# Up projections of a two-layer encoder: the first unit of every group makes its high products in eights ahead of its low ones, not in pairs with them

## The chip, the cores and the metric

One core of one Trainium2 chip runs the whole program. The metric is the device time of one execution in microseconds (us); smaller is better. Products run on TensorE (PE in the profile), weight loads on the same engine beside them (PEld), the other work on VectorE (DVE), ScalarE (ACT) and GpSimd (POOL), and SyncE (SP) issues nearly all DMAs.

## The reference

The input is x (1, 256, 2048) in float32, with a condition c and parameters of two layers. Per layer: a norm, modulated by c, an input projection that feeds four mixers, an output projection, a post-norm, and then a gated feed-forward part. Only that last part is touched:

```
h = layer_norm(x) * (1.0 + scale_f) + shift_f
up = h @ w_up[l]                       # (256, 2048) @ (2048, 2 * 5632)
gate, val = split(up, 2)
gate = causal_dwconv(gate, w_conv, b_conv)   # width 3
y = (silu(gate) * val) @ w_down[l]
x = layer_norm(ALPHA * x + (1.0 + gate_f) * y, ...)
```

The up projection has 11264 columns per layer over 2048 rows; it is 42% of the kernel's span.

## The kernel before, in words

**High and low parts.** A float32 weight is used as two float32r parts: a high part, made by an ACT cast (line 344), and a low part, what is left, made by a DVE subtraction (line 345, which reads the high part). The activations hT are split in the same way. One weight block of 128 rows x 128 columns gives two products (both through the helper at line 117): a *high product*, the high weights with 512 moving columns (256 tokens of the high activations beside 256 of the low ones), and a *low product*, the low weights with the 256 high activations. Both add into one accumulator of PSUM.

**Groups and units.** `group2` makes 512 output columns: four accumulators c0 to c3 of 128 channels each, summed over 16 blocks of rows. A group has four *units* of four row blocks: one DMA of 1 MB (tile wraw, 4 buffers), then two *tiles* of two row blocks each, so two casts (whi, 4 buffers) and two subtractions (wlo, 4 buffers), then 16 high and 16 low products. With four buffers of each and two a unit, the casts and subtractions of a unit two further on wait until PE has read the tiles of this one for the last time.

**The stage.** `ffn_up` makes gate groups (g_c in the profile) and value groups (v_c) in turn, 10 gate groups (the first gate group of a layer is made otherwise, by `first_group`) and 11 value groups in each of the two layers: 42 groups. A layer's input projection uses `group2` too, in layer 1 alone, and there with `apart=True`: groups Dg, Da, U, Cc, Ch, E. Units are issued in a software pipeline (`stream`): the loads, casts and subtractions of a unit are written ahead of the products of the one before. The Tile framework's scheduler then orders each engine's instructions by its own estimate of when they can start; PE, DVE and ACT then run their own instructions in that order.

**Order of products in a unit.** Without `apart`, a unit makes two halves, c0 and c1 first, then c2 and c3, and in a half each high product is followed by its low one: high, low, high, low, eight of each. With `apart`, unit 0 makes the same two halves, but in each the eight high products and then the eight low ones; its later units make all sixteen high ones and then all sixteen low ones.

**What else runs beside it.** When a group has ended, ACT copies half of each accumulator out (line 1391) and DVE adds the other half (1398 or 1428). Gate groups put a convolution (line 1420) and a SiLU (1423) in the background. In layer 0, DVE also multiplies the modulation weights of later steps (tile wmod, line 193, 2.3 us each). Near the end of a layer's up projections the gated activations are split for the down projection (lines 365 and 366, tile a), whose products are called d.

Of the kernel before, what the change touches and what calls it, by code (L numbers as in the profile page):

```python
# [86 lines left out]
def encoder_kernel(ctx: ExitStack, tc: tile.TileContext, A: dict, consts: bass.AP, out: bass.AP):  # L87
# [25 lines left out]
    def acc_tile(name):  # L113
        return accp.tile([P, 512], F32, tag="acc", name=name)

    def mm(o, lhsT, rhs, start, stop):
        pe.matmul(o, lhsT, rhs, start=start, stop=stop, skip_group_check=True)  # L117
# [196 lines left out]
    def weights(w, k0, nk, c0, width, exact=False, spare=0):  # L314

        w, l = w
        n = nk * width
        if exact:
            parts, per = [], min(nk, max(1, 1024 // width))
            for k in range(0, nk, per):  # L320
                if spare:
                    r = slot("wexact")
                else:
                    tag = ("whi", "wlo")[exact_turn[0] % 2]
                    exact_turn[0] += 1
                    r = splitp.tile([P, 1024], F32, tag=tag, name="wexact")
                m = per * width
                nc.sync.dma_start(out=r[:, :m], in_=w.take(m, rows_of(l, k0 + k, per, c0, width)))
                for j in range(per):
                    parts.append((r[:, j * width : (j + 1) * width], None))  # L330
            return parts
        raw = raw_tile("wraw")
        nc.sync.dma_start(out=raw[:, :n], in_=w.take(n, rows_of(l, k0, nk, c0, width)))
        per = max(1, 1024 // width)
        parts = []
        for k in range(0, nk, per):
            m = per * width
            if k < spare:
                hi, lo = slot("thi", F32R), slot("tlo", F32R)
            else:  # L340
                hi = splitp.tile([P, 1024], F32R, tag="whi", name="whi")
                lo = splitp.tile([P, 1024], F32R, tag="wlo", name="wlo")
            r = raw[:, k * width : k * width + m]
            held(act.copy(hi[:, :m], r), "cast")  # L344
            i = dve.tensor_tensor(out=lo[:, :m], in0=r, in1=hi[:, :m].bitcast(F32), op=ALU.subtract)  # L345
            held(i, "split")
            for j in range(per):
                parts.append((hi[:, j * width : (j + 1) * width], lo[:, j * width : (j + 1) * width]))
        return parts
# [69 lines left out]
    def group2(w, c0, name, then, bg=0, spare=0, apart=False):  # L419


        nk = 4
        box = {}

        def products(item, u):
            if u == 0:
                box["c"] = [acc_tile(f"{name}_c{i}") for i in range(4)]
                box["h"] = list(hT)
            if apart:
                for part in (range(0, 2), range(2, 4)) if u == 0 else (range(0, 4),):  # L430
                    for low in (0, 1):
                        for k, w_k in enumerate(item):
                            kt = u * nk + k
                            both = box["h"][kt // 2][2][:, kt % 2, :, :]
                            for i in part:
                                o, a = box["c"][i], w_k[low][:, i * P : (i + 1) * P]
                                if low:
                                    mm(o[:, :S], a, both[:, 0, :], False, kt == KT - 1)
                                else:
                                    mm(o, a, both.rearrange("p h t -> p (h t)"), kt == 0, False)  # L440
                return
            for part in (range(0, 2), range(2, 4)):
                for k, (hi, lo) in enumerate(item):
                    kt = u * nk + k
                    both = box["h"][kt // 2][2][:, kt % 2, :, :]
                    for i in part:
                        o = box["c"][i]
                        off = slice(i * P, (i + 1) * P)
                        mm(o, hi[:, off], both.rearrange("p h t -> p (h t)"), kt == 0, False)
                        mm(o[:, :S], lo[:, off], both[:, 0, :], False, kt == KT - 1)  # L450

        def load(u):
            return weights(w, u * nk, nk, c0, 512, False, spare if u == 0 else 0)

        return KT // nk, load, products, lambda: then(box["c"]), bg

    def latent_group(w, c0, name, then, hF=None, bg=0):
# [1201 lines left out]
```

## Time and profile before

| | |
|---|---|
| median of 3 runs | 2212.66 us (2212.3, 2212.66, 2218.01) |
| profiled execution | 2212.3 us, span of its instructions 2210.5 us |
| mean granted TensorE clock | 0.996 |
| PE busy | 2184.5 us (99% of the span), 10852 matmuls |
| PEld busy | 1792.5 us (81%) |
| DVE busy | 1701.8 us (77%) |
| ACT busy | 1076.1 us (49%) |
| HBM | 604.17 MB read, 274 GB/s over the span |

How to read it: the ends of matmuls are modelled, and a matmul is shown longer than the time until the next one starts. So what a product costs is read from the distance between the starts of runs of products (the chain and the timeline), not from the mean duration of one. A few matmul records are missing, which merges two neighbours in the timeline and moves no start of a run that is recorded.

### The profile page before, as it was taken

The numbers are of one execution on the slowest core, as the hardware profiler recorded it, in microseconds if no ns is written. First come the engines' busy times: TensorE is split into PE (matmuls) and PEld (weight loads), VectorE is DVE, ScalarE is ACT, GpSimd is POOL, SyncE is SP. The second block draws the span as 40 slices with busy tenths as digits, with TensorE's granted clock in tenths as the row PEclk, the third lists the DMA queues.
The fourth block names the chain that finished last, engine by engine and source line by source line (L and its number), as shares of the span: only waits on it lengthen the run. The fifth ranks groups of instructions, "written<-read, shape, count | busy, mean of one in ns | idle before, by whom it ended". The sixth has DMA issues, their size and how long they took to land. (4 is left out here: it accounts for less than half of the span.)

```text
span 2210.5 us, 28322 instructions
## 1 busy us (share of the span) xinstructions
PE 2184.5 (99%) x10852; PEld 1792.5 (81%) x10852; DVE 1701.8 (77%) x2265; ACT 1076.1 (49%) x1652; POOL 21.9 (1%) x38
## 2 busy tenths in 40 slices
PE   8999999999999999999999999999999999999997
PEld 6776865588888888888877988868888888888886
DVE  5657997798898888989968988877765656575776
ACT  3132730655454545545665455465444544454553
POOL 0000000000000000000000000000000000000000
PEclk9999999999999999999999999999999999999999
DMA  9999889598888988898857547856765555565553
GB/s 392 417 375 391 353 331 392 214 343 322 334 315 319 327 326 318 335 342 325 285 218 304 184 153 263 326 195 245 267 210 190 188 191 191 191 210 192 192 196 144
DMA packets 94730, 608.15 MB, mean 275 GB/s; under 512 B 10689, under 2 KB 10881, under 8 KB 29313
## 3 DMA queue, kind: packets, MB, share of 16 engines
q1 hardware_dynamic: 94466, 606.31, 74.3%
q8 instruction: 85, 1.39, 0.2%
q14 instruction: 51, 0.42, 0.0%
q10 hardware_dynamic: 128, 0.03, 0.0%
HBM read 604.17 MB, written 2.13 MB: 274 GB/s over the span
## 5 line engine op out<-in xcount | busy, mean ns | idle before, releaser
L345 DVE TENSOR_TENSOR wlo<-wraw,whi 128x1024 fp32r<-128x1024 f32 (+1 forms) x608 | 728.5, 1212 | 294.4 <-ACT whi L344 279.2
L344 ACT CAST whi<-wraw 128x1024 fp32r<-128x1024 f32 (+1 forms) x608 | 631.5, 1045 | 637.0 <-PE g_c L117 214.2
L117 PE MATMUL v_c<-hT,whi 128*128 128x512 f32 x1408 | 489.2, 392 | 0.0
L193 DVE SCALAR_TENSOR_TENSOR wmod<-wmod,crep 128x2048 f32<-128x2048 f32 x192 | 438.0, 2285 | 59.6 <-DMA wmod<-in_w_mod_dram 58.9
L117 PE MATMUL g_c<-hT,whi 128*128 128x512 f32 x1280 | 444.6, 392 | 0.0
L117 PE MATMUL v_c<-hT,wlo 128*128 128x256 f32 x1408 | 392.1, 279 | 0.0
L117 PE MATMUL d<-whi,a 128*128 128x512 f32 x1344 | 386.4, 389 | 0.0
L117 PE MATMUL g_c<-hT,wlo 128*128 128x256 f32 x1280 | 356.5, 278 | 0.0
L117 PEld LDWEIGHTS v_c<-hT,whi 128*128 128x128 f32 x1408 | 263.6, 187 | 59.1
L117 PEld LDWEIGHTS d<-whi,a 128*128 128x128 f32 x1344 | 252.0, 188 | 52.3
L117 PEld LDWEIGHTS g_c<-hT,whi 128*128 128x128 f32 x1280 | 239.7, 187 | 54.1
L117 PEld LDWEIGHTS v_c<-hT,wlo 128*128 128x128 f32 x1408 | 265.3, 188 | 0.1
L117 PEld LDWEIGHTS g_c<-hT,wlo 128*128 128x128 f32 x1280 | 241.1, 188 | 0.0
L117 PE MATMUL d<-wlo,a 128*128 128x512 f32 x672 | 232.9, 389 | 0.0
L117 PEld LDWEIGHTS d<-wlo,a 128*128 128x128 f32 x672 | 126.1, 188 | 26.3
L365 ACT CAST a<-g 128x512 fp32r<-128x512 f32 x132 | 81.3, 617 | 63.7 <-PE d L117 63.1
L366 DVE TENSOR_TENSOR a<-g,a 128x512 fp32r<-128x512 f32 x132 | 88.7, 684 | 5.1 <-ACT a L365 5.1
L117 PE MATMUL o<-whi,a 128*128 128x512 f32 x320 | 91.1, 391 | 0.0
L503 PE MATMUL first<-wexact,hN 128*128 128x512 f32 x192 | 85.5, 596 | 0.5
L1420 DVE SCALAR_TENSOR_TENSOR u<-g,par,u 128x254 f32<-128x254 f32 (+1 forms) x176 | 73.8, 476 | 0.0
L117 PEld LDWEIGHTS o<-whi,a 128*128 128x128 f32 x320 | 59.9, 188 | 12.8 <-ACT whi L344 0.4
L503 PEld LDWEIGHTS first<-wexact,hN 128*128 128x128 f32 x192 | 35.3, 190 | 40.3 <-issue 35.2
(311 smaller groups left out, 2171.8 us busy)
## 6 DMA issues: line engine op xcount, KB each, us to landing
wmod<-in_w_mod_dram SPq DMA_DIRECT2D x192, 1024.0 KB, 7.1
wraw<-in_ffn_w_up_dram SPq DMA_DIRECT2D x168, 1024.0 KB, 5.1
wraw<-in_ffn_w_down_dram SPq DMA_DIRECT2D x88, 1024.0 KB, 4.9
wexact<-in_w_in_dram SPq DMA_DIRECT2D x64, 512.0 KB, 11.3
wraw<-in_w_in_dram SPq DMA_DIRECT2D x24, 1024.0 KB, 6.8
wraw<-in_w_out_dram SPq DMA_DIRECT2D x22, 1024.0 KB, 5.7
wexact<-in_w_out_dram SPq DMA_DIRECT2D x20, 512.0 KB, 11.6
wexact<-in_ffn_w_up_dram SPq DMA_DIRECT2D x16, 512.0 KB, 5.4
```

Source lines behind the costliest of these rows:

```text
L117: pe.matmul(o, lhsT, rhs, start=start, stop=stop, skip_group_check=True)
L193: i = dve.scalar_tensor_tensor(out=raw, in0=raw, scalar=1.0, in1=crep, op0=ALU.mult, op1=ALU.mult, accum_out=col)
L344: held(act.copy(hi[:, :m], r), "cast")
L345: i = dve.tensor_tensor(out=lo[:, :m], in0=r, in1=hi[:, :m].bitcast(F32), op=ALU.subtract)
L365: last_cast[0] = act.copy(hi, src).ins.name
L366: dve.tensor_tensor(out=lo, in0=src, in1=hi.bitcast(F32), op=ALU.subtract)
L503: i = pe.matmul(ps, hN[kt // 4][:, kt % 4, t * P : (t + 1) * P], parts[kt], start=kt == 0, stop=kt == KT - 1, skip_group_check=True,)
L1420: dve.scalar_tensor_tensor(out=u[:, sh:], in0=x[:, : S - sh], scalar=col(k, j), in1=u[:, sh:], op0=ALU.mult, op1=ALU.add)
```

## The change

One condition. In `group2`, the branch that makes high products ahead of low ones is taken in unit 0 of every group, also where `apart` is off. Only the up projections call `group2` with `apart` off, so in their 42 groups unit 0 goes from pairs to eight high and eight low products, twice. Units 1 to 3 of these groups stay in pairs. The number of instructions, their operands and all DMAs stay.

```
@@ -426,7 +426,7 @@
             if u == 0:
                 box["c"] = [acc_tile(f"{name}_c{i}") for i in range(4)]
                 box["h"] = list(hT)
-            if apart:
+            if apart or u == 0:
                 for part in (range(0, 2), range(2, 4)) if u == 0 else (range(0, 4),):
                     for low in (0, 1):
                         for k, w_k in enumerate(item):
```

On PE, in the second half of unit 0 of the second gate group of layer 0: whi_2545 and wlo_2546 are the high and low parts of the unit's first tile, whi_2549 the high part of its second one, and c2 and c3 are accumulators.

```order
 L117 MATMUL g01_c2_2614<-hT_2326,whi_2545 128x512
+L117 MATMUL g01_c3_2615<-hT_2326,whi_2545 128x512
+L117 MATMUL g01_c2_2614<-hT_2326,whi_2545 128x512
+L117 MATMUL g01_c3_2615<-hT_2326,whi_2545 128x512
+L117 MATMUL g01_c2_2614<-hT_2327,whi_2549 128x512
+L117 MATMUL g01_c3_2615<-hT_2327,whi_2549 128x512
+L117 MATMUL g01_c2_2614<-hT_2327,whi_2549 128x512
+L117 MATMUL g01_c3_2615<-hT_2327,whi_2549 128x512
 L117 MATMUL g01_c2_2614<-hT_2326,wlo_2546 128x256
-L117 MATMUL g01_c3_2615<-hT_2326,whi_2545 128x512
 L117 MATMUL g01_c3_2615<-hT_2326,wlo_2546 128x256
-L117 MATMUL g01_c2_2614<-hT_2326,whi_2545 128x512
```

All eight high products now stand ahead of the first low one; so PE is done with the two high tiles earlier in the unit than before, and with the first low tile later.

On DVE, in layer 0, where it makes the low parts of the third gate group (g02): wlo_3058 and wlo_3062 are the two low tiles of that group's unit 2, which take over buffers that unit 0 has read, and wmod is a multiplication of modulation weights.

```order
 L345 TENSOR_TENSOR wlo_3058<-wraw_3055,whi_3057 128x1024
+L345 TENSOR_TENSOR wlo_3062<-wraw_3055,whi_3061 128x1024
 L193 SCALAR_TENSOR_TENSOR wmod_3097,sums_0_5_2367<-wmod_3097,crep_104 128x2048
-L345 TENSOR_TENSOR wlo_3062<-wraw_3055,whi_3061 128x1024
 L345 TENSOR_TENSOR wlo_3103<-wraw_3100,whi_3102 128x1024
```

One subtraction moves ahead of one multiplication. The rest of DVE's order is the same but for one more such exchange, with a split of activations near the end of layer 1.

On ACT, near the end of layer 1's up projections: whi_15459 is the second high tile of unit 2 of the last value group, a_15656 a part of the activations of the down projection, and g_15376 a SiLU of the gate.

```order
 L344 CAST whi_15455<-wraw_15453 128x1024
-L365 CAST a_15656<-g_11857 128x2x256
+L344 CAST whi_15459<-wraw_15453 128x1024
 L1423 ACTIVATE g_15376<-u_15443 128x256
 L1423 ACTIVATE g_15376<-u_15448 128x256
-L344 CAST whi_15459<-wraw_15453 128x1024
+L365 CAST a_15656<-g_11857 128x2x256
 L365 CAST a_15693<-g_11857 128x2x256
```

The cast moves ahead of two SiLUs, and the first split of the activations behind them. A handful of other groups have a cast exchanged with a SiLU in the same way. The orders of POOL and SP are unchanged.

More of the change, by code (lines that the diff above doesn't have):

```diff
@@ L428, in products @@
                 box["h"] = list(hT)
-            if apart:
+            if apart or u == 0:
                 for part in (range(0, 2), range(2, 4)) if u == 0 else (range(0, 4),):
```

## The prediction

> **What bounds the kernel now.** I read the page first, for the busy shares; PE is busy in 99% of the span and no other engine passes 77%.
>
> ```profile
> span 2210.5 us, 28322 instructions
> PE 2184.5 (99%) x10852; PEld 1792.5 (81%) x10852; DVE 1701.8 (77%) x2265; ACT 1076.1 (49%) x1652; POOL 21.9 (1%) x38
> ```
>
> A busy share doesn't say whether PE waits in the stage that is changed, so next comes the chain that ended last, in order of time. From 1492.59 us it is PE almost without a break; these are some of the pieces of layer 1's up projections (start, length, what).
>
> ```profile
> 1515.46 22.19 PE g_c L117 x128
> 1537.64 22.19 PE v_c L117 x128
> ...
> 1914.82 22.19 PE g_c L117 x128
> 1937.01 22.19 PE v_c L117 x128
> 1959.19 0.11 PE ps_gate L239
> 1959.30 239.42 PE d L117 x1056
> ```
>
> Every group takes the same 22.19 us, whatever DVE and ACT did meanwhile, and each starts when the one before ends. That is a stage in which PE sets the time and waits for nobody. For both layers I checked it by the stages' windows (length, busy time of PE, PEld, DVE, ACT, POOL, granted clock, DMA share, GB/s): PE is busy in 466.99 of 467.00 us in layer 0, too, where DVE and the DMAs have more to do, and the clock is full.
>
> ```profile
> 433.00:900.00 467.00, 466.99 (x2696) 408.11 (x2695) 412.97 (x510) 244.15 (x349) 0.00 (x0) 1.00 0.89 326
> 1493.00:1959.00 466.00, 466.00 (x2691) 410.92 (x2691) 301.50 (x407) 241.72 (x346) 0.00 (x0) 1.00 0.60 208
> ```
>
> The costliest groups give the same for high and low products apart; the number behind the last bar is the idle time ahead of the instructions.
>
> ```profile
> L345 DVE TENSOR_TENSOR wlo<-wraw,whi 128x1024 fp32r<-128x1024 f32 (+1 forms) x608 | 728.5, 1212 | 294.4 <-ACT whi L344 279.2
> L344 ACT CAST whi<-wraw 128x1024 fp32r<-128x1024 f32 (+1 forms) x608 | 631.5, 1045 | 637.0 <-PE g_c L117 214.2
> L117 PEld LDWEIGHTS v_c<-hT,whi 128*128 128x128 f32 x1408 | 263.6, 187 | 59.1
> L117 PEld LDWEIGHTS g_c<-hT,whi 128*128 128x128 f32 x1280 | 239.7, 187 | 54.1
> L117 PEld LDWEIGHTS v_c<-hT,wlo 128*128 128x128 f32 x1408 | 265.3, 188 | 0.1
> L117 PEld LDWEIGHTS g_c<-hT,wlo 128*128 128x128 f32 x1280 | 241.1, 188 | 0.0
> ```
>
> Two things are to be seen. The loads of low weights never wait: 0.1 us over all 2688 of them. And the waiting goes the other way: ACT's casts wait for PE (214.2 us for g_c alone), and DVE's subtractions wait for the casts. The 113.2 us ahead of the high loads have no releaser and are 42 ns each: a load that is through early and waits for the long product before it. The counts also give the number of units: 2688 high products, 64 to a group, are 42 groups.
>
> **The change, part by part.** A pair now costs 22.19 us / 64 = 346.7 ns. The down products, which are all of 512 columns, cost 239.42 us / 1056 = 226.7 ns each; so a low product of 256 columns has 120.0 ns of the pair.
>
> *Products in runs.* What eight high and eight low ones in a row cost, layer 1's input projection shows already, since its groups do in their unit 0 just what the change asks for. This is the timeline of PE over group U (start, length, run): its unit 0 is the four runs of eight, then come units of sixteen and sixteen.
>
> ```profile
> 1214.86 2.08 PE L117 MATMUL Da_c<-hT,wlo 128*128 128x256 f32 x16
> 1216.78 2.00 PE L117 MATMUL U_c<-hT,whi 128*128 128x512 f32 x8
> 1218.62 1.12 PE L117 MATMUL U_c<-hT,wlo 128*128 128x256 f32 x8
> 1219.57 2.00 PE L117 MATMUL U_c<-hT,whi 128*128 128x512 f32 x8
> 1221.41 1.11 PE L117 MATMUL U_c<-hT,wlo 128*128 128x256 f32 x8
> 1222.36 3.82 PE L117 MATMUL U_c<-hT,whi 128*128 128x512 f32 x16
> 1226.02 2.08 PE L117 MATMUL U_c<-hT,wlo 128*128 128x256 f32 x16
> 1227.93 3.82 PE L117 MATMUL U_c<-hT,whi 128*128 128x512 f32 x16
> ```
>
> From start to start, unit 0 takes 1222.36 - 1216.78 = 5.58 us, a unit in pairs 22.19 / 4 = 5.55 (5.5475). Eight high products take 1.84 us (230 ns each, 3 above the down products' 226.7), eight low ones 0.95 (119 each). So the runs cost about 0.03 us more a unit. The next unit, sixteen and sixteen, takes 1227.93 - 1222.36 = 5.57 with half as many turns from low to high; the excess of about 0.02 us seems to hang on that turn. I take 0.02 for a turn, 0.04 for a unit with two: 42 x 0.04 = 1.7 us. Unit 0 read directly gives 42 x 0.0325 = 1.4. Both ends hang on two decimals, and I take 1.6, all of it on the path, since PE has no gap that could swallow it.
>
> *A rule that bears on it.* In the run of lows, the load of the next weights has only a low product to hide behind; the rows above give a load 188 ns, more than the 120 that such a product takes. In the Trainium skill, the page TensorE: Matmul & The Clock Gate, section LDWEIGHTS (loading the stationary operand), puts a load at columns / 1.2 ns, an estimate of 107 ns for 128 columns, which just fits behind a low product; by it the sum stays as it is. By the duration in the row it would grow as the second rival below works out. The trace agrees with the rule: sixteen lows in a row took 1216.78 - 1214.86 = 1.92 us, 120 ns each, so 188 ns isn't the spacing of loads.
>
> *What goes.* The one thing that the new order can take away is a wait of the first low product for its subtraction: in unit 0 the first low now comes after eight highs, 8 x 0.23 - 0.23 = 1.6 us later. The rows have 0.1 us of such waiting in all. Gain: 0 to 0.1 us; I take 0.
>
> *What is released at another time.* Count from the start of unit 0. Before, the second half starts at 2.77; PE is done with the low tiles at 2.77 + 4 x 0.347 = 4.16 and at 5.55, and with the high tiles 0.12 ahead of that, 4.04 and 5.43. After, the second half starts at 2.79, its highs end at 3.70 (first tile) and 4.63 (second), its lows at 5.11 and 5.58. So the high tiles come free 0.3 and 0.8 us earlier, the second low tile at the same time, and the first low tile 0.95 us later. The unit that takes over these buffers is unit 2. In layer 1's last group, whose first product starts at 1936.84, ACT and DVE show this handover; the third row is the first load of unit 2's low weights.
>
> ```profile
> 1941.08 1.05 ACT L344 CAST whi<-wraw 128x1024 fp32r<-128x1024 f32 x1 [0.21 <-PE v_c L117]
> ...
> 1942.72 1.22 DVE L345 TENSOR_TENSOR wlo<-wraw,whi 128x1024 fp32r<-128x1024 f32 x1
> ...
> 1936.84 0.39 PE L117 MATMUL v_c<-hT,whi 128*128 128x512 f32 x1
> ...
> 1947.94 0.19 PEld L117 LDWEIGHTS v_c<-hT,wlo 128*128 128x128 f32 x1
> ```
>
> The low tile comes free at 1936.84 + 4.16 = 1941.00 now and would at 1941.95 after; the subtraction starts only at 1942.72, because DVE is at other work and the cast has to run first. So the later release stays covered, by 0.8 us. And if it were not, the subtraction ends at 1943.94 and is wanted at 1947.94: 4.0 us to spare. Behind the subtraction on DVE stand the unit's second one and, in layer 0, a wmod multiplication; nobody on PE waits for the latter. The least to spare is in layer 0's first group, where four subtractions run in a row.
>
> ```profile
> 444.38 4.62 DVE L345 TENSOR_TENSOR wlo<-wraw,whi 128x1024 fp32r<-128x1024 f32 x4
> 445.93 0.42 PEld L117 LDWEIGHTS v_c<-hT,wlo 128*128 128x128 f32 x2
> 434.72 0.39 PE L117 MATMUL v_c<-hT,whi 128*128 128x512 f32 x1
> ```
>
> The first of the four belongs to unit 2 and ends at 444.38 + 1.21 = 445.6, 0.3 us ahead of its load at 445.93. Its low buffer comes free at about 439.5 after (unit 0 starts 0.35 ahead of the third row's product, and 434.4 + 5.1 = 439.5), five microseconds ahead of 444.38. Cost: 0, at most 0.95 - 0.3 = 0.6 us if I have the place wrong.
>
> *The moved casts and subtractions.* These are a pair of SiLUs on ACT, beside which a cast is moved, and the first split of the activations for the down projection, which moves behind such a pair.
>
> ```profile
> 445.12 0.71 ACT L1423 ACTIVATE g<-u 128x256 f32<-128x256 f32 x2
> 1942.04 0.61 ACT L365 CAST a<-g 128x512 fp32r<-128x512 f32 x1
> ```
>
> A cast that changes places with SiLUs comes 0.7 us earlier or later, and its tile is done microseconds before its use. The split is cast at 1942.04 and wanted by the down products, from 1959.30 on. Both 0. SP's queue, and so the DMAs, stay as they were; a raw tile is released by its subtraction, at about the same time as before.
>
> *Sum.* 2212.3 (profiled execution) + 1.6 - 0 + 0 = 2213.9 us: 2212.1 us of span and the 1.8 that lie around it. The profiled execution is the lowest of the three runs and 0.4 us below their median; I forecast 2214.0, 0.06% above the median. About 0.3%, 6.6 us, is what a measurement of this kernel can tell from no change.
>
> **The rivals.**
>
> *Faster: lows that come late.* If PE did wait for subtractions in unit 0, 1.6 us could go in each of 42 groups, 67 us, 2146 us. Against it stands the 0.1 us of idle time ahead of low loads and the even 22.19 us. For a gain past 6.6 us there would have to be (6.6 + 1.6) / 42 = 0.2 us of waiting in a group, and there is none. Chance 0.02.
>
> *Slower: the loads set the pace in the run of eight lows.* Place: the seven intervals inside each run, 84 runs. Price: 188 - 120 = 68 ns each, 7 x 84 x 0.068 = 40 us, 2254 us. It decides where a load takes longer than the product before it. Against it stand the runs of lows of groups Da and U, at 120 ns. What speaks for it is only that those groups ran beside less DMA and DVE work than layer 0's up stage. Chance 0.03.
>
> *Slower: DVE is held by the low tile that comes free later.* If the subtraction of unit 2 had been waiting for just that buffer, it and all behind it would come 0.95 us later; where the subtractions have nothing to spare, this is PE's loss, at most 42 x 0.95 = 40 us, 2254 us. The rows give 4.0 us to spare in the last group and 0.3 in layer 0's first, where the buffer isn't what is waited for. So mostly 0, in one group 0.6 us. Chance of more than 6.6 us: 0.02.
>
> *Nothing is moved.* The scheduler could have undone the edit. PE's order shows the runs of eight in all 42 groups, so this is out, and its time (2212.7) would lie within the forecast's range anyhow.
>
> **How the numbers follow.** The forecast, a loss of 0 to 1.7 us and within 0.3%, has the rest, 0.93. Faster 0.02; slower 0.03 + 0.02 = 0.05. The range: the sum's ends are 2212.2 (no cost, 0.1 us gained) and 2212.3 + 1.7 + 0.6 = 2214.6; the three runs lie 5.7 us apart, and I put half of that, 2.9, on either side: 2209.3 to 2217.5. The rivals' 0.07 stays outside.
>
> **What would show it.** In the changed kernel's chain, the groups g_c and v_c should take 22.22 to 22.23 us in place of 22.19, all alike, and the timeline of their unit 0 should show runs of eight, highs 1.84 us and lows 0.95 from start to start. The idle time ahead of low loads should stay under 1 us. DVE's subtractions may show small waits for PE that they don't show now. Wrong would be: a group time that varies, lows at more than 125 ns in a run, PE waiting for DVE in unit 2, or the stage from 1493 us on shorter than 466 us.

## The result, and the profile after

The changed kernel is slower: 2227.7 us, median of 6 runs, against 2212.76 us for 6 runs of the kernel before; the ratio is 1.0065, with a 95% interval of 1.0055 to 1.0075. The forecast was 2214.0 and no change that can be told; the loss is some 15 us in place of 1.6, and lies outside the range.

The page after has nearly the same shares, and a span 14.6 us longer; PE's busy time has grown by the same 14.6 us. So PE is as closely busy as before, and its products take longer.

```profile
span 2225.1 us, 28321 instructions
PE 2199.1 (99%) x10852; PEld 1799.4 (81%) x10852; DVE 1703.1 (77%) x2265; ACT 1070.2 (48%) x1652; POOL 21.9 (1%) x38
```

The chain has the place. Every group of the up projections takes 22.55 us, where it took 22.19; the down products are unchanged.

```profile
1522.74 22.55 PE g_c L117 x128
1545.28 22.55 PE v_c L117 x128
...
1951.12 22.55 PE v_c L117 x128
...
1973.78 239.40 PE d L117 x1056
```

41 groups x 0.36 us are 14.8 us, as much as the span has grown. The timeline of PE over one group tells where in the group it arises. It shows unit 0 as four runs, then the first pairs of unit 1 (start, length, product).

```profile
1522.57 2.00 PE L117 MATMUL g_c<-hT,whi 128*128 128x512 f32 x8
1524.41 1.12 PE L117 MATMUL g_c<-hT,wlo 128*128 128x256 f32 x8
1525.37 2.00 PE L117 MATMUL g_c<-hT,whi 128*128 128x512 f32 x8
1527.21 1.11 PE L117 MATMUL g_c<-hT,wlo 128*128 128x256 f32 x8
1528.16 0.40 PE L117 MATMUL g_c<-hT,whi 128*128 128x512 f32 x1
1528.39 0.28 PE L117 MATMUL g_c<-hT,wlo 128*128 128x256 f32 x1
1528.51 0.40 PE L117 MATMUL g_c<-hT,whi 128*128 128x512 f32 x1
...
1532.05 0.40 PE L117 MATMUL g_c<-hT,whi 128*128 128x512 f32 x1
...
1534.87 0.40 PE L117 MATMUL g_c<-hT,whi 128*128 128x512 f32 x1
```

Unit 0 takes 1528.16 - 1522.57 = 5.59 us, as forecast. It is the pairs behind it, whose order did not change, that got slower: from 1528.51 to 1534.87 are 18 pairs, 353 ns each. Before, the same group's pairs went like this.

```profile
1521.88 0.39 PE L117 MATMUL g_c<-hT,whi 128*128 128x512 f32 x1
1522.11 0.28 PE L117 MATMUL g_c<-hT,wlo 128*128 128x256 f32 x1
...
1523.96 0.39 PE L117 MATMUL g_c<-hT,whi 128*128 128x512 f32 x1
```

Six pairs in 1523.96 - 1521.88 = 2.08 us, 347 ns each. For sharper numbers I take a unit's time from the start of its first weight load to that of the next unit's: 32 loads each, in ns. In one group of layer 1 the four units take 5579, 5653, 5658 and 5657 after, and 5546 or 5547 each before. Unit 0 has lost 32 ns, units 1 to 3 about 110 each. The spacing inside, from the start of one product to that of the next, also has another pattern: before, 230 ns from a high start to the low one and 116 or 117 on to the next high, pair after pair; after, 236, 113, 233, 117, 241, 120, over and over: 1060 ns for three pairs, 353.3 each in place of 346.7. The granted clock is 0.996 in both.

Loads of low weights have some idle time ahead of them now, without a releaser.

```profile
L117 PEld LDWEIGHTS v_c<-hT,wlo 128*128 128x128 f32 x1408 | 247.6, 189 | 3.6
L117 PEld LDWEIGHTS g_c<-hT,wlo 128*128 128x128 f32 x1280 | 225.1, 189 | 3.1
```

That is 6.7 us over 2688 loads, not enough for 14.6, and in the second experiment below it is absent while the loss is there.

### The profile page after: what moved, and what is told of

It is laid out like the page before. It is cut to its first block, busy times and chain, and to the rows that moved or that the text cites. A ratio compares the mean times of both kernels' runs of the same rounds, so it can differ in the third digit from the quotient of the medians.

```text
span 2225.1 us, 28321 instructions
## 1 busy us (share of the span) xinstructions
PE 2199.1 (99%) x10852; PEld 1799.4 (81%) x10852; DVE 1703.1 (77%) x2265; ACT 1070.2 (48%) x1652; POOL 21.9 (1%) x38
## 5 line engine op out<-in xcount | busy, mean ns | idle before, releaser
L117 PE MATMUL v_c<-hT,whi 128*128 128x512 f32 x1408 | 462.7, 397 | 0.0
L117 PE MATMUL g_c<-hT,whi 128*128 128x512 f32 x1280 | 420.3, 397 | 0.0
L117 PE MATMUL v_c<-hT,wlo 128*128 128x256 f32 x1408 | 345.3, 281 | 0.0
L117 PE MATMUL g_c<-hT,wlo 128*128 128x256 f32 x1280 | 314.2, 281 | 0.0
L117 PEld LDWEIGHTS v_c<-hT,wlo 128*128 128x128 f32 x1408 | 247.6, 189 | 3.6
L117 PEld LDWEIGHTS g_c<-hT,wlo 128*128 128x128 f32 x1280 | 225.1, 189 | 3.1
```

## Experiments

**Theories.** A: a *rhythm*. The same pairs can go at 346.7 or at 353.3 ns; a run of low products leaves PE in the slow rhythm, and it stays there until something breaks it. B: the *changed unit's own cost*. The buffers that unit 0 frees at other times, and the casts and subtractions that they let run beside the products, slow the units behind. B is the kind of effect that the prediction had looked for.

All experiments but the fourth use one helper in place of the branches of `group2`; it gives each half of a unit a list of turn lengths. A turn of n is n highs, then their n lows; `[1] * 8` is pairs and `[8]` the changed order. All but the last were run once each, so the times of the units, which come again to 1 or 2 ns from group to group, carry more than the totals. The helper, cut where `...` stands, with the changed order written in it:

```
+        def runs(u):
+            if apart:
+                return ((range(0, 2), [8]), (range(2, 4), [8])) if u == 0 else ((range(0, 4), [16]),)
+            first, second = [8] if u == 0 else [1] * 8, [8] if u == 0 else [1] * 8
+            return (range(0, 2), first), (range(2, 4), second)
...
+            for part, lengths in runs(u):
+                steps = [(k, i) for k in range(nk) for i in part]
+                for n in lengths:
+                    for low in (0, 1):
+                        for k, i in steps[:n]:
...
+                    del steps[:n]
```

**Runs in the first half alone.**

```
-            first, second = [8] if u == 0 else [1] * 8, [8] if u == 0 else [1] * 8
+            first, second = [8] if u == 0 else [1] * 8, [1] * 8
```

> Only the first half of each group's unit 0 is in runs of eight; its second half and units 1 to 3 are in pairs. Theory A, a rhythm: after a run of low products, the pairs that follow go at 353.4 ns in place of 346.7 until something breaks the rhythm. Then 8 + 48 pairs of a group are slow: 42 x (56 x 0.0067 + 0.02) = 16.6 us, about 2229 us, and units 1 to 3 take 5.65 us. Theory B, the changed unit's own cost: the buffers that come free at other times, and with them the casts and subtractions beside the products, slow the units behind. Here the second half, which releases the buffers, is as before: most of the loss should go, 2213 to 2220 us, and units 1 to 3 take 5.55 to 5.60 us.

Measured: 2228.1 us beside 2211.72 of the kernel before; units of 5606, 5657, 5645 and 5658 ns. One group of the chain:

```profile
1523.66 22.57 PE g_c L117 x128
```

By its groups (22.57 us in place of 22.55), half the edit costs a little more than the whole, as A has it: there are eight more pairs to be slow. The second half, which releases the buffers, is in pairs as before, and ACT and DVE run in the order of the kernel before, so neither of these is the cause.

**Runs in one unit of a layer.**

```
-            first, second = [8] if u == 0 else [1] * 8, [8] if u == 0 else [1] * 8
+            first, second = [8] if u == 0 and name in ("g01", "g11") else [1] * 8, [8] if u == 0 and name in ("g01", "g11") else [1] * 8
```

> Runs of eight in one unit of a layer only: unit 0 of the second gate group. All else is in pairs as in the kernel before, and the orders of ACT and DVE are those of before. Theory A: the slow rhythm stays over all groups behind that unit to the end of the layer's up projections, (48 + 19 x 64) pairs x 0.0067 = 8.5 us a layer, so about 2229 us, more than with all 42 units changed, and groups of 22.6 us with no run in them. Theory B: two of 42 units, 15 x 2 / 42 = 0.7 us, about 2213.4 us; the groups behind take 22.19 us.

Measured: 2228.51 us beside 2211.72. This is the chain in layer 1; the unit in runs is the first of the second group.

```profile
1501.21 21.96 PE v_c L117 x127
1523.17 22.55 PE g_c L117 x128
1545.71 22.61 PE v_c L117 x128
...
1930.15 22.61 PE g_c L117 x128
1952.76 22.61 PE v_c L117 x128
```

To be seen: one unit of 32 products is changed in each layer, and twenty groups, up to 450 us later, are slow, those without a run more (22.61) than the one with it. Two changed units cost as much as 42. ACT and DVE run in the order of the kernel before, so B is out, and the loss hasn't to do with which unit is changed but with what is left behind it. In this kernel the idle time ahead of low loads is nearly that of before (0.4 us in all, 0.1 before), and the slow pairs are there all the same.

```profile
L117 PEld LDWEIGHTS v_c<-hT,wlo 128*128 128x128 f32 x1408 | 266.0, 189 | 0.1
L117 PEld LDWEIGHTS g_c<-hT,wlo 128*128 128x128 f32 x1280 | 240.1, 189 | 0.3
```

**A turn of two behind the runs.**

```
+            first, second = [8] if u == 0 else [2] + [1] * 6 if u == 1 else [1] * 8, [8] if u == 0 else [1] * 8
```

> As the changed kernel, but the first two pairs of unit 1 are made high, high, low, low, as at one place of layer 0's first group, behind which the pairs were fast again. ACT's and DVE's orders are those of the changed kernel. Theory A: the rhythm is broken at that place, units 1 to 3 take about 5.55 us again (unit 1 perhaps 0.05 more), and 42 x (0.04 to 0.1) = 2 to 4 us are left: 2214 to 2217 us. Theory B: as the changed kernel, 2227 to 2228 us, units 1 to 3 at 5.65.

Measured: 2214.41 us beside 2211.72. The chain, and the timeline at the turn:

```profile
1516.94 22.21 PE g_c L117 x128
1539.15 22.21 PE v_c L117 x128
```

```profile
1521.40 1.11 PE L117 MATMUL g_c<-hT,wlo 128*128 128x256 f32 x8
1522.35 0.63 PE L117 MATMUL g_c<-hT,whi 128*128 128x512 f32 x2
1522.82 0.39 PE L117 MATMUL g_c<-hT,wlo 128*128 128x256 f32 x2
1523.05 0.40 PE L117 MATMUL g_c<-hT,whi 128*128 128x512 f32 x1
...
1525.82 0.40 PE L117 MATMUL g_c<-hT,whi 128*128 128x512 f32 x1
```

Eight pairs from 1523.05 to 1525.82 take 346 ns each; the units take 5562, 5558, 5547 and 5546. Exchanging two products, in the place where the slow pairs would start, takes away nearly all of the loss, with all 42 units still in runs, and ACT and DVE in the order of the changed kernel.

**All units in runs.**

```
-            if apart:
+            if apart or True:
```

> All four units of the up groups in runs, eight and eight in unit 0 and sixteen and sixteen in units 1 to 3, as the layer 1 input projection has them. Theory A: there are no pairs to be slow; five turns of 0.02 us a group, 42 x 0.1 = 4.2 us, about 2217 us; groups of 22.29 us. Theory B: four times as many units are changed, so at least as slow as the changed kernel, 2227 us or more.

Measured: 2216.82 us beside 2211.72; units of 5587, 5567, 5566 and 5567 ns.

```profile
1517.76 22.29 PE g_c L117 x128
1540.05 22.29 PE v_c L117 x128
```

Four times the change costs a third of it, since no pairs are left to be slow. Group U of the kernel before, by its weight loads, has units of the same 5587, 5566 and 5567 ns. So the loss is not in the runs: it takes pairs behind them.

**How long a turn, and from which rhythm.**

```
+            one, n = [1] * 8, (2 * int(name[2:]) - (name[0] == "g")) % 8 + 1
+            turn, two = [n] + [1] * (8 - n), [2] + [1] * 6
+            first = ([8], turn, one, one)[u] if name[1] == "0" else ([8], two, turn, one)[u]
+            second = [8] if u == 0 else one
```

> Unit 0 of every up group in runs of eight, as in the changed kernel; behind it one turn of n highs and n lows, then pairs, with n from 1 to 8 by the group's place. In layer 0 the turn opens unit 1, where the pairs would be slow; in layer 1 unit 1 opens with a turn of two, which should make the pairs fast, and the turn of n opens unit 2. Read are the times of the units behind the turn: 5.55 us fast, 5.65 slow. Theory A1, the last run of lows decides alone: a run of three or more lows, whose spacing has settled at 120 ns, leaves slow pairs, a shorter one fast pairs. Then in both layers n = 2 gives 5.55 behind it and n of 3 to 8 gives 5.65; n = 1 is an ordinary pair and leaves things as they are, slow in layer 0 and fast in layer 1. Theory A2, the rhythm met by the turn counts as well: the same n gives different units in the two layers; in the kernel with the turn in unit 1, a turn in layer 0's first group seems to have made fast pairs slow, so n = 2 would then be slow in layer 1.

Measured: 2220.7 us beside 2211.92. The chain in layer 1, groups in turn with n = 2 to 8 and 1; the last one here has n = 1.

```profile
1519.57 22.42 PE g_c L117 x128
1541.99 22.43 PE v_c L117 x128
1564.42 22.40 PE g_c L117 x128
1586.82 22.44 PE v_c L117 x128
1609.26 22.41 PE g_c L117 x128
1631.67 22.38 PE v_c L117 x128
1654.05 22.42 PE g_c L117 x128
1676.46 22.23 PE v_c L117 x128
```

The time of the unit of pairs behind the turn's unit, in ns, the same to 1 or 2 ns wherever that n comes again (but for n = 1 in layer 0's first group, where the scheduler has a turn of its own in that unit):

| n | 1 | 2 | 3 | 4 | 5 | 6 | 7 | 8 |
|---|---|---|---|---|---|---|---|---|
| layer 0, turn right behind the run of eight | 5658 | 5546 | 5546 | 5547 | 5656 | 5658 | 5645 | 5657 |
| layer 1, turn among fast pairs | 5547 | 5656 | 5659 | 5645 | 5657 | 5658 | 5645 | 5656 |

For n = 3 in layer 0, the timeline has eight pairs from 485.62 to 488.39, 346 ns each:

```profile
484.21 0.86 PE L117 MATMUL v_c<-hT,whi 128*128 128x512 f32 x3
484.91 0.52 PE L117 MATMUL v_c<-hT,wlo 128*128 128x256 f32 x3
...
485.62 0.39 PE L117 MATMUL v_c<-hT,whi 128*128 128x512 f32 x1
...
488.39 0.39 PE L117 MATMUL v_c<-hT,whi 128*128 128x512 f32 x1
```

A1 falls: turns of three or four lows leave fast pairs where the changed kernel has slow pairs, and two are enough to make fast pairs slow. A2 holds: what follows a turn hangs on the turn and on what it met. Here turns of two to four leave fast pairs behind a run of eight and slow pairs behind fast pairs; turns of five and more end in the slow rhythm. For n = 2 this is not a matter of the layer, as the third experiment has it behind the run in both layers, with fast pairs after it; for 3 and 4 the layer and the place were changed together.

Fast and slow are not the whole of what a turn can meet, and the kernel before shows it. In layer 0's first group, in unit 2, the scheduler had written three highs and then two lows (and two lows once more later), among fast pairs:

```profile
445.46 0.86 PE L117 MATMUL v_c<-hT,whi 128*128 128x512 f32 x3
446.16 0.39 PE L117 MATMUL v_c<-hT,wlo 128*128 128x256 f32 x2
446.39 0.40 PE L117 MATMUL v_c<-hT,whi 128*128 128x512 f32 x1
```

There that unit takes 5561 ns and the pairs behind it stay fast (5547). In the third experiment the same order in the same place, also among fast pairs, leaves slow pairs: 5629, then 5658. The fast pairs differed in their spacing: 230 and 117 ns over and over before, and 231, 112, 233, 117 in the third experiment, behind its turn of two. Both come to 346.7 ns a pair. So these turns are no recipe: what one does has to be read from the trace of its own place.

**Turns of two and of four throughout.**

```
+            first, second = [2] * 4 if name[1] == "0" else [4] * 2, [2] * 4 if name[1] == "0" else [4] * 2
```

> All four units of the up groups in turns of two highs and two lows in layer 0, of four and four in layer 1; no pairs anywhere. Is there an order that is faster than pairs? Theory A: a product has the same floor in every order, 120 ns for a low and 226.7 for a high one, and a turn costs up to 0.02 us on top: groups of 22.2 us or more in both layers, at most 22.8 (32 turns of 0.02), nothing under 22.19; in all 2213 to 2230 us. Against it would be a group under 22.1 us.

Measured: 2220.13 us beside 2211.92; units of 5573 or 5574 ns in layer 0 (a group of 22.29 us), 5613 or 5614 in layer 1.

```profile
1517.90 22.45 PE g_c L117 x128
1540.36 22.45 PE v_c L117 x128
```

No order tried is under the 22.19 us of fast pairs, so there is no version here that beats the kernel before. The price of a turn isn't one number either: eight turns of two add 27 ns to a unit, four turns of four add 67.

**Another product between runs and pairs.**

```
+            if u == 1 and not apart:
+                pe.matmul(ms_tile("spare")[:, :P], ident, ident, start=True, stop=True, skip_group_check=True)
```

> The changed kernel with one more small product, 128x128 of the constants into a spare accumulator, ahead of unit 1 of each up group. Theory A: any product of another kind between the run of lows and the pairs may break the slow rhythm, as the transposes ahead of layer 1's first pairs leave fast ones; then units 1 to 3 take 5.55 us and the kernel 2212.7 + 1.7 + 42 x 0.1 to 0.25 for the products themselves = 2219 to 2225 us. If the rhythm stays, units 2 and 3 take 5.65 and the time is 2232 to 2238 us.

Measured: 2235.51 us beside 2211.92. Unit 0 with the added product takes 5.80 us, units 1 to 3 5648, 5645 and 5658 ns: the rhythm is slow still. "Anything breaks it" is wrong; this product, at least, doesn't.

**Longer low products.** Each adds a part of the low weights times the low activations, so the result has a term more than the kernel's.

```
+            first, second = ([8], [8]) if u == 0 and name[0:3:2] != "v0" else ([1] * 8, [1] * 8)
...
+                                m = S if apart else 512 if name[1] == "0" else 320
+                                mm(o[:, :m], a, both.rearrange("p h t -> p (h t)")[:, :m], False, kt == KT - 1)
```

> Low products are made longer: 512 moving columns in layer 0 and 320 in layer 1 in place of 256, which adds the low weights times the low activations (all of it, or a quarter), so the result has a small term more. Unit 0 in runs of eight in every group but the first value group of a layer, whose pairs come ahead of any run. Theory L: the slow rhythm can arise because a low product of 120 ns is hardly longer than the load of the next weights takes; with longer lows there is room and the rhythm is gone: units 1 to 3 behind runs take what the first group's take, 16 x 453.3 = 7.25 us in layer 0 and 16 x (226.7 + 146.7) = 5.97 us in layer 1, to within 0.02. Theory M: the rhythm belongs to the alternation of long and short products or of two weight tiles as such, whatever the lows' length: in layer 1 at least, units behind runs take 0.05 to 0.1 us more than those of the first group. Both: about 2213 + 143 + 36 = 2392 us.

> As the kernel before, with low products of 384 columns in layer 0 and 288 in layer 1 (each again with a part of the low weights times the low activations added). Theory L: at 384 columns no unit behind runs is slower than the first group's, 16 x (226.7 + 173.3) = 6.40 us; at 288 columns, 13 ns longer than a low product is now, the rhythm is gone or nearly so, 16 x (226.7 + 133.3) = 5.76 us. Theory M: in both, units behind runs take 0.05 to 0.1 us more. About 2213 + 72 + 18 = 2303 us.

Measured: 2399.03 and 2321.47 us beside 2212.19, the median of the kernel before on that chip; 7 and 18 us over what was expected. Units 2 and 3, in pairs, in ns, in the first group (ahead of any run) and behind runs, beside an estimate of what the products cost alone. The estimate puts lengths on a line through the 120.0 ns of 256 columns and the 226.7 of 512. In the runs of eight of these kernels, lows of 288 and 320 columns are 132 and 146 ns apart on average, near the line (133.3 and 146.7), and those of 384 are 178 apart, above its 173.3:

| low columns | 288 | 320 | 384 | 512 |
|---|---|---|---|---|
| first group | 5813 | 6080 | 6613 | 7253 |
| behind runs | 5813 | 6080 | 6613 | 7253 |
| estimate, 16 x (226.7 + 13.3 + columns x 106.7 / 256) | 5760 | 5973 | 6400 | 7253 |

Neither theory is right as put. M falls: at none of these lengths does it matter what went before. L's first half stands, that there is no second rhythm; its second half falls: except at 512, pairs take 3.3 to 13.3 ns more than the estimate for their products, in the first group as well. The chain at 320 columns shows a group with a run beside the plain sum, 4 x 5.97 = 23.9 us:

```profile
1661.21 24.25 PE g_c L117 x128
1685.46 24.25 PE v_c L117 x128
```

So at the three other unequal lengths a pair costs more than the estimate for its parts, and the 346.7 ns of the kernel before, which equal the parts, are the exception among the lengths tried: at 256 columns pairs go without that cost, or with 6.7 ns of it, as much as at 320.

**The turn of two, timed.** The kernel with runs in unit 0 and the turn of two in unit 1 again, in three rounds.

> The kernel with runs of eight in unit 0 and a turn of two at the start of unit 1, timed in three rounds. Theory A: the units behind are fast, and only the runs and the turn themselves remain, 42 x 0.027 = 1.1 us by its trace: 0.05 to 0.15% slower than before, which can't be told from no change.

Measured: 2214.02 us, against 2212.19 before; ratio 1.0006, interval 0.9996 to 1.0015. It can't be told from no change. This is what the forecast said of the change: the runs by themselves, here with the turn of two behind them, cost as little as worked out.

## Why the prediction was wrong

*What bounds the kernel*: right. PE sets the time, the idle time ahead of the low loads has no other engine as its releaser, and all of the loss is PE's own.

*Products in runs*: right in size, and in its last digit by luck. Unit 0 was put at 0.04 us more, a read of 0.0325 beside it; it is 0.032. 42 of them are 1.3 us. But this too hangs on what stands ahead: the same unit in runs costs 0.037 us in the second experiment and 0.015 in the third, both behind fast pairs, 0.040 in the fourth, behind runs, and up to 0.060 in the fifth.

*A rule that bears on it*: right in what it was used for; lows in a run are 119 to 120 ns apart.

*What goes*: right, nothing. *What is released at another time* and *the moved casts and subtractions*: right that they cost nothing; the second experiment has the loss without them.

*The step that failed* stands in the first sentence of the change's part: "a pair now costs 22.19 us / 64 = 346.7 ns". I took that as a property of the pair and used it for units 1 to 3 after the change, which have no line in the sum at all, because they "stay in pairs". It is a property of the pair and of what went before it. The runs show 353.3 ns a pair in these units in its place. The sum lacked 126 units x 0.11 us = 13.9 us, less 0.2, as layer 0's first group falls back into the fast rhythm in its unit 2, where the scheduler's own order has three highs and two lows in a row. With the 1.3 us of unit 0 that makes 15.0, and the medians lie 14.9 apart.

Could it have been seen? The spacing of 22.19 us was so even that I read it as the one price there is; but every group in the trace that has pairs came in the fast rhythm, and every group with runs had no pairs behind them in its own units. The trace of before had no pairs behind a long run of lows, so it could not price them; the one place with two lows in a row, in layer 0's first group, left fast pairs and so gave no warning. That was a missing row, to be bounded from both sides, and I did not look for it: among the "units that stay" I saw nothing to bound. The nearest bound was at hand: a turn from low to high cost 0.02 us in group U, and if each of 16 pairs in a unit had paid a third of such a turn, the loss would have been of this size.

*The rivals*: "the loads set the pace" and "DVE is held" both end slower, but by mechanisms that didn't occur. The chance of slower, 0.05, was too small: it counted only mechanisms that I had thought of, in a change that touches 42 places on the one engine without slack.

*What would show it*: the chain's group time, forecast at 22.22 to 22.23, did show it at a glance, and the idle time ahead of low loads, forecast at under 1 us, came to 6.7. None of the signs listed as wrong came: the groups are all alike, only slower, and the list had no line for that. The small waits of DVE for PE that were named are there, from the waits of the kernel after (total, times, longest), and cost nothing:

```profile
DVE wlo L345 <- PE g_c L117: 14.3, 8, 1.8
```

What stays open is what in PE makes the two rhythms. The runs show that it isn't the operands' arrival (in the second experiment low loads wait 0.4 us in all), the granted clock (0.996 before and after) or ACT's and DVE's order; that the rhythm lasts over hundreds of microseconds of pairs; and that two rhythms were seen with lows of 256 columns and only one with 288, 320, 384 or 512. Whether it is the loads of weights or the reading of the moving columns that slips was not separated.

## What to carry to other kernels

On an engine without slack, the time of an instruction stream need not be the sum of its products' prices: time what comes behind a changed stretch too, and look at its spacing, not only at the stretch itself. When a reorder of a few instructions costs more than they take, compare the start-to-start pattern far behind them, and test with the edit made once: if that costs as much as everywhere, the cost is a state and not the edit. Mixing two orders of the same products can be dearer than either alone.

## What the runs showed of the hardware

- High and low products in pairs, 512 and 256 columns, run at 346.7 or 353.3 ns a pair on the same operands and at the same granted clock, and stayed slow for 20 groups (450 us) behind one unit in runs. In the Trainium skill, TensorE: Matmul & The Clock Gate, section Back-to-back issue gap, says that in a stream of loads and products the spacing comes from both; no run here separates the two. Its formula for an isolated gap would give an estimate of 325 ns for the pair (512 / 2.4 + 2.5 and 256 / 2.4 + 2.5), which no order here reached; the measurement decides.
- A turn of two to four highs and lows left fast pairs (5546 or 5547 ns a unit) behind a run of eight and slow pairs (5645 to 5659) behind fast pairs of one pattern of spacing; five to eight ended in the slow rhythm. The same turn in the same surroundings gave the same time to 1 or 2 ns at each repetition, but the scheduler's three highs and two lows ended fast (5547) behind one pattern of fast pairs and slow (5658) behind the other.
- Pairs with a low product of 288, 320 and 384 columns take 3.3, 6.7 and 13.3 ns more than the estimate for the two products alone; with 512 nothing. At 384, a unit in runs of eight took 6544 ns and one in pairs 6613: there runs are the faster order.
